# A hybrid encoder layer on one core: first modulation on TensorE, normalisation on three engines, K and Q sums on VectorE, the residual gate 16 chunks later

## The chip, the core and the metric

The kernel runs on one core of a Trainium2 chip. The metric is the device time of one execution in microseconds (us). Five engines work in parallel, each through its own stream of instructions in a fixed order: TensorE (PE in the profile: matrix products; PEld: its weight loads), VectorE (DVE), ScalarE (ACT), GpSimd (POOL), and SyncE (SP), which here only issues DMA transfers. An instruction that waits holds up everything behind it on its engine. Products land in PSUM, 8 banks of 128x512 floats, and a bank must be emptied by VectorE or ScalarE before it is used again.

## The reference

```python
mod = jax.nn.silu(c) @ w_ada[l] + b_ada[l]
shift, scale, gate = jnp.split(mod[:, None, :], 3, axis=-1)
h = _layernorm(x) * (1.0 + scale) + shift
proj = h @ w_in[l]
u, v, z_a, q, k, v_b, z_b = jnp.split(proj, IN_SPLITS, axis=-1)
y_a = _spatial_gating(gelu(u), gelu(v), z_a, ...)   # u * (W_s LN(v) + b) * silu(z_a), 8 groups of 128
y_b = _neighbourhood_attention(q, k, v_b, rpb) * silu(z_b)   # 16 heads of 64
y = jnp.concatenate([y_a, y_b], axis=-1) @ w_out[l]
x = _layernorm(DEEPNORM_ALPHA * x + (1.0 + gate) * y, ln_g[l], ln_b[l])
```

There are 512 tokens, a model width of 2048, and one layer. `w_ada` is 2048x6144, `w_in` 2048x7168, `w_out` 2048x2048, all float32, so that some 126 MB of weights are read once.

## The kernel before, in words

Every float32 weight tile and every activation is split into a rounded part and a rest (`hi` and `lo`), and one product becomes three: hi·hi, hi·lo and lo·hi (`mm3`, line 206). A weight *chunk* is 128x1024 floats (two k tiles of 128 rows by 512 columns): its DMA fills `raw`, ScalarE casts `whi` (line 192), and VectorE or GpSimd subtracts to get `wlo` (line 194). One chunk feeds 24 matmuls of 512 columns, or, for the values and their gate (`VZ`), 24 of 256 columns (line 235) and 12 of 512.

All chunks stand in one list, `plan`, in the order of their use. `pump()` issues their DMAs on SP's queue ahead of use, as long as there is room among 4 `raw` buffers; `split_w()` takes the next one and issues cast and subtraction. The same list holds 32 integers, the *gate steps*: a 128x1024 block of the third part of `w_ada` is loaded into one of two `rawg` buffers, and VectorE adds c times it to `gate1` (line 178). `gate1` is summed over partitions much later (`gate_sum`) and is needed first by the output projection.

The program is staged as follows.

- **Start.** Four token tiles of x are normalised (`first_norm`): VectorE takes statistics, GpSimd computes the factors and scales four quarters (line 412), TensorE transposes them, ScalarE copies them back.
- **Preparation beside the first segments.** For each k tile, `ada_dve` multiplies blocks of `w_ada` (`wada`, six buffers) with c on VectorE (lines 351 and 353), sums the two halves (ScalarE line 357, VectorE line 358), lets TensorE sum over partitions with a column of ones (line 364), and `make_h` forms `h_hi` and `h_lo` (lines 374 to 379). The first two k tiles are done singly, the others in pairs. `advance` deals out these steps among the products by a fixed pace.
- **Segments.** `SEGMENTS` lists k pairs 0, 1, 2, 3, {4,5} and {6,7}. In each, five column groups are worked on: V, U, ZA, VZ0 and KQ0. VZ0 stays in four PSUM banks (`res`); the other groups' partial sums go from two PSUM banks (ring "x") into SBUF with `sum_evac`: for V and U by VectorE (line 440), for ZA and KQ0 by a ScalarE copy (line 437) into a quarter of `gate1` that serves as scratch, and a GpSimd addition (line 438).
- **Last segment**, k pairs {6,7}, in the order KQ0, V, U, VZ0, ZA, with four new banks of ring "x". Beside it runs `sgu`, the spatial gating of the first half: VectorE statistics of V, GpSimd's `rss` (line 119), a scaling (line 524), two GpSimd operations (526, 527), products (533) and VectorE's two operations on their result (534, 537).
- **Three head quarters** q = 1, 2, 3: 16 chunks each, beside the attention of the quarter before. Then V, U and ZA of the second half (24 chunks), the second spatial gating and `gate_sum`, and 32 chunks of the output projection with the final layer norm.

`run(main, side, pace, start)` sets how the side work is dealt out among the products. Below that a scheduler may move an instruction ahead of others on its engine, unless it is wrapped in `pin`, which keeps it in program order. The gate steps begin at plan index 40, the first head quarter, and are spread as 2 per 3 chunks; their VectorE operation is not pinned.

Of the kernel before, what the change touches and what calls it, by code (L numbers as in the profile page):

```python
# [8 lines left out]
F32 = mybir.dt.float32  # L9
F32R = mybir.dt.float32r  # L10
AF = mybir.ActivationFunctionType
# [28 lines left out]

AHEAD, PER_PAIR = 16, 16

LASTS = [0, 0, 1, 1, 1, 1, 1, 0, 1, 0]

PACE_FIRST = (1.5, 18)
# [23 lines left out]
def hybrid_kernel(ctx: ExitStack, tc: tile.TileContext, x, c, w_ada, b_ada_cols, b_gate, w_in,  # L69
# [99 lines left out]
    def split_w():  # L169
# [137 lines left out]
    with tc.tile_pool(name="ph1", bufs=1) as ph1:  # L307
# [32 lines left out]
        def ada_dve(k0, nk):  # L340

            w = nk * P
            step = 4 // nk
            part = [t[:, :2 * w].rearrange("p (s w) -> p s w", s=2) for t in acc_ps]
            for j0 in range(0, NK, step):
                wt = ada_next()
                for j in range(j0, j0 + step):
                    cj = c_sb[:, j:j + 1]
                    acc = part[j % 2]
                    if j < 2:  # L350
                        nc.vector.tensor_scalar(out=acc, in0=wt[:, j - j0], scalar1=cj, scalar2=None, op0=ALU.mult)
                    else:
                        nc.vector.scalar_tensor_tensor(out=acc, in0=wt[:, j - j0], scalar=cj, in1=acc, op0=ALU.mult, op1=ALU.add)  # L353
                pump()
                yield
            even, both = [scratch[i][:, :2 * w].rearrange("p (s w) -> p s w", s=2) for i in range(2)]
            nc.scalar.copy(out=even, in_=part[0])
            nc.vector.tensor_tensor(out=both, in0=part[1], in1=even, op=ALU.add)

            pc = acc_ps[0][:, T - 2:] if nk == 1 else bank()[:, :2 * nk]  # L360
            pc = pc.rearrange("p (s k) -> p s k", s=2)
            for s in range(2):
                for i in range(nk):
                    nc.tensor.matmul(pc[:, s, i:i + 1], lhsT=both[:, s, i * P:(i + 1) * P], rhs=one, start=True, stop=True)
            nc.vector.tensor_tensor(out=modc[:, :, k0:k0 + nk], in0=pc, in1=bada[:, :, k0:k0 + nk], op=ALU.add)
            yield

# [13 lines left out]
        def prepare():  # L381
            for k0, nk in ada_groups:
                yield from ada_dve(k0, nk)
                for kk in range(k0, k0 + nk):
                    make_h(kk, k0 < 2)
                    yield
# [8 lines left out]
        rstd = ph1.tile([P, NT], F32, name="rstd")  # L395
        for n in range(NT):
# [3 lines left out]
        def first_norm(n):  # L400
# [8 lines left out]
            nc.gpsimd.tensor_tensor(out=rstd[:, n:n + 1], in0=rstd[:, n:n + 1], in1=mhalf[:, 0:1], op=ALU.pow)  # L409
            for q in range(4):  # L410
# [19 lines left out]
        def sum_evac(q, i, ps, first):  # L430

            acc = accs[q][0][i]
            if first:
                nc.scalar.copy(out=acc, in_=ps)
            elif q in (ZA, KQ0):
# [6 lines left out]
        def sums(q, wls, i, first):  # L442
# [7 lines left out]
            sum_evac(q, i, ps, first)  # L450
            yield

        def first_segment():
# [11 lines left out]
            for i in range(2):  # L465
                mm3(two[i], wv, i, 1, False, False, True)
                sum_evac(V, i, two[i], True)
                yield
            for i in range(2, 4):
                yield from sums(V, [wv], i, True)  # L470
# [486 lines left out]
```

## Time and profile before

| | |
|---|---|
| median of 3 runs | 963.13 us (961.21 to 964.08) |
| the profiled execution | 963.75 us, its span 962.0 us |
| mean granted TensorE clock | 0.974 of 2.4 GHz |
| busy: PE, DVE, ACT, POOL | 881.7, 592.9, 337.3, 363.5 us |
| read from HBM | 140.6 MB |

Times in the rows below are microseconds from the start of the span. "Idle before" names what ended an engine's wait. A matmul's recorded duration overlaps the next one's, so the distance of starts is the cost of one in a row of many. PEclk is the granted TensorE clock; it has two levels, 1.2 and 2.4 GHz, and a value between is the mean over a stretch.

### The profile page before, as it was taken

How to read it: one execution, taken by the hardware profiler on the slowest of the kernel's cores; microseconds unless marked ns; L12 is line 12 of the kernel's file. 1: busy time of each engine (PE TensorE's matmuls, PEld its weight loads, DVE VectorE, ACT ScalarE, POOL GpSimd, SP SyncE). 2: the span in 40 equal slices, each digit the busy share in tenths (PEclk: the TensorE clock that was granted, in tenths of full speed). 3: DMA queues.
4: the chain of work that ended last, by engine and by line, in shares of the span. 5: the costliest groups of instructions: out<-in, count | busy, mean ns of one | idle time of the engine just before them, and what ended most of it. 6: DMA issues, size and time to landing. Idle time of an engine off the chain costs nothing.

```text
span 962.0 us, 11759 instructions
## 1 busy us (share of the span) xinstructions
PE 881.7 (92%) x4408; PEld 760.7 (79%) x4408; DVE 592.9 (62%) x834; ACT 337.3 (35%) x426; POOL 363.5 (38%) x271
## 2 busy tenths in 40 slices
PE   3699998997985997899999999999999999999994
PEld 3588787886874986689988998899888888888883
DVE  7748768621987875757455745574847843342657
ACT  3364343333531214172516251624245432122300
POOL 5435786367472143434424342434235000000035
PEclk9799999999997998999999999999999999999998
DMA  9969789734626665323233223333232374223313
GB/s 308 311 219 355 243 259 301 239 88 131 197 75 217 205 214 176 99 88 99 89 97 97 91 88 99 88 88 88 75 101 88 115 274 180 89 86 110 110 44 131
DMA packets 107787, 145.59 MB, mean 151 GB/s; under 512 B 6993, under 2 KB 78801, under 8 KB 106961
## 3 DMA queue, kind: packets, MB, share of 16 engines
q1 hardware_dynamic: 103120, 134.25, 43.8%
q10 hardware_dynamic: 4610, 10.59, 3.2%
q8 instruction: 34, 0.56, 0.2%
q14 instruction: 23, 0.19, 0.1%
HBM read 140.62 MB, written 4.19 MB: 151 GB/s over the span
## 4 chain that ended last, share of the span: by engine, by line
PE 57%; DVE 7%; DMA 4%; POOL 3%; issue 2%; ACT 1%; POOLq 0%; DVEq 0%; ACTq 0%
PE psm L222 47%; PE psm L235 5%; DMA rawg<-in_w_ada_dram 4%; DVE gate L178 3%; PE psx L222 1%; DVE s L524 1%; POOL xr L836 1%; POOL xr L837 1%; PE psx L654 1%; PE psx L605 1%; PE psx L606 1%; PE psx L652 1%; DVE wlo L194 1%; PE psx L653 1%; PE psx L533 1%
## 5 line engine op out<-in xcount | busy, mean ns | idle before, releaser
L192 ACT CAST whi<-raw 128x1024 fp32r<-128x1024 f32 x133 | 139.5, 1049 | 328.6 <-PE psm L222 239.6
L194 DVE TENSOR_TENSOR wlo<-raw,whi 128x1024 fp32r<-128x1024 f32 x94 | 126.8, 1349 | 175.4 <-ACT whi L192 172.3
L222 PE MATMUL psm<-h_hi,whi 128*128 128x512 f32 x444 | 175.6, 396 | 0.0
L222 PE MATMUL psm<-h_lo,whi 128*128 128x512 f32 x444 | 174.9, 394 | 0.0
L222 PE MATMUL psm<-h_hi,wlo 128*128 128x512 f32 x444 | 174.5, 393 | 0.0
L194 POOL TENSOR_TENSOR wlo<-raw,whi 128x1024 fp32r<-128x1024 f32 x39 | 94.8, 2437 | 96.6 <-ACT whi L192 80.6
L222 PE MATMUL psm<-whi,h_hi 128*128 128x512 f32 (+1 forms) x296 | 114.7, 388 | 0.0
L222 PE MATMUL psm<-wlo,h_hi 128*128 128x512 f32 (+1 forms) x296 | 114.0, 385 | 0.0
L222 PE MATMUL psm<-whi,h_lo 128*128 128x512 f32 (+1 forms) x296 | 114.0, 385 | 0.0
L222 PEld LDWEIGHTS psm<-h_hi,wlo 128*128 128x128 f32 x444 | 84.5, 190 | 18.2
L222 PEld LDWEIGHTS psm<-h_lo,whi 128*128 128x128 f32 x444 | 84.7, 191 | 15.1
L222 PEld LDWEIGHTS psm<-h_hi,whi 128*128 128x128 f32 x444 | 84.3, 190 | 15.4 <-ACT s L775 0.2
L353 DVE SCALAR_TENSOR_TENSOR ada<-wada,c_sb,ada 128x512 f32<-128x512 f32 (+1 forms) x126 | 79.8, 688 | 19.8 <-DMA wada<-in_w_ada_dram 16.5
L222 PE MATMUL psx<-h_hi,whi 128*128 128x512 f32 x160 | 65.5, 411 | 11.3 <-ACT gate L437 7.8
L119 POOL TENSOR_TENSOR rs<-vareps,mhalf 128x1 f32<-128x1 f32 x4 | 4.4, 1099 | 184.5 <-DVE vareps L118 184.5
L235 PE MATMUL psm<-whi,h_lo 128*128 128x256 f32 x248 | 71.2, 289 | 2.8 <-DVE h_lo L379 2.8
L235 PE MATMUL psm<-wlo,h_hi 128*128 128x256 f32 x248 | 71.1, 287 | 2.7 <-POOL wlo L194 1.9
L235 PE MATMUL psm<-whi,h_hi 128*128 128x256 f32 x248 | 71.4, 288 | 2.4 <-ACT h_hi L374 2.3
L222 PEld LDWEIGHTS psm<-wlo,h_hi 128*128 128x128 f32 x296 | 63.6, 215 | 8.4
L222 PEld LDWEIGHTS psm<-whi,h_lo 128*128 128x128 f32 x296 | 63.4, 214 | 8.5
L222 PEld LDWEIGHTS psm<-whi,h_hi 128*128 128x128 f32 x296 | 63.4, 214 | 8.5
L222 PE MATMUL psx<-h_hi,wlo 128*128 128x512 f32 x160 | 63.5, 397 | 2.3 <-POOL wlo L194 2.3
(196 smaller groups left out, 1668.7 us busy)
## 6 DMA issues: line engine op xcount, KB each, us to landing
wada<-in_w_ada_dram SPq DMA_DIRECT2D x128, 256.0 KB, 5.7
raw<-in_w_in_dram SPq DMA_DIRECT2D x128, 256.0 KB, 3.2
raw<-in_w_in_dram SPq DMA_DIRECT2D x48, 512.0 KB, 3.8
rawg<-in_w_ada_dram SPq DMA_DIRECT2D x32, 512.0 KB, 4.4
raw<-in_w_out_dram SPq DMA_DIRECT2D x32, 512.0 KB, 3.7
xt<-in_x_dram SPq DMA_DIRECT2D x8, 512.0 KB, 8.6
xr<-in_x_dram ACTq DMA_DIRECT2D x4, 1024.0 KB, 9.0
tt<-in_rpb_dram ACTq DMA_DIRECT2D x16, 128.0 KB, 2.5
```

What stands on the lines that cost most here:

```text
L178: nc.vector.scalar_tensor_tensor(out=gate1[:, cs], in0=raw, scalar=c_sb[:, j:j + 1], in1=gate1[:, cs], op0=ALU.mult, op1=ALU.add)
L192: nc.scalar.copy(out=hi, in_=raw)
L194: eng.tensor_tensor(out=low, in0=raw, in1=hi.bitcast(F32), op=ALU.subtract)
L222: nc.tensor.matmul(ps, lhsT=a, rhs=b, start=first and j == 0, stop=last and j == 2)
L235: nc.tensor.matmul(ps[:, t * w:(t + 1) * w], lhsT=a, rhs=b[:, cs], start=first and t == 0 and j == 0, stop=last and t == 1 and j == 2)
L353: nc.vector.scalar_tensor_tensor(out=acc, in0=wt[:, j - j0], scalar=cj, in1=acc, op0=ALU.mult, op1=ALU.add)
L524: nc.vector.tensor_scalar(out=v[n][:, tok(g)], in0=v[n][:, tok(g)], scalar1=mvs[:, g, 0:1], scalar2=rs[:, g:g + 1], op0=ALU.subtract, op1= ...
L533: nc.tensor.matmul(ps[:, tok(n)], lhsT=v[n][:, tok(g)], rhs=wsT[:, g, :], start=True, stop=True)
L605: nc.tensor.matmul(po, lhsT=k2[:, h, keys], rhs=q2[:, h, q], start=True, stop=False)
L606: nc.tensor.matmul(po, lhsT=klo[:, h, keys], rhs=q2[:, h, q], start=False, stop=True)
L652: nc.tensor.matmul(ps[:, q], lhsT=v_hi[:, t, h, :], rhs=hi[:, sl], start=t == 0, stop=False, skip_group_check=True)
L653: nc.tensor.matmul(ps[0:64, q], lhsT=v_lo[:, t, h, :], rhs=hi[:, sl], start=False, stop=False, skip_group_check=True)
```

## The change

1. The first two k tiles' modulation goes to TensorE: `ada_tensor` multiplies each 128x128 block of `w_ada`, as stationary operand, with one column of c, 32 matmuls for each k tile, and VectorE adds the bias straight from PSUM. For the other pairs, `ada_vector` lets the last multiply-add of the even half write SBUF (no ScalarE copy), and the end of one pair (`ada_end`: sum over partitions, `make_h`) comes after the first or second block of the next.
2. `first_norm`'s four quarters go to GpSimd, ScalarE, VectorE and GpSimd (for the last tile VectorE takes the fourth too); GpSimd computes one more factor, `nb`.
3. `sum_evac`: KQ0 is added by VectorE, ZA too in segment 4.
4. The gate steps begin at plan index 56, in place of 40, and are inserted after the second half's chunks are in the plan, so that 48 chunks carry them: those of head quarters 2 and 3, and of V and U. Their VectorE operation is pinned.
5. `pump()` keeps 3 `raw` tiles loaded and not yet split, in place of 4; there are still 4 buffers.
6. `sgu` in the last segment takes PSUM banks of ring "m" in place of "x"; paces and the interleaving at the start (`LASTS`) are set anew.

```diff
+FIRST_GATE = 56
-LASTS = [0, 0, 1, 1, 1, 1, 1, 0, 1, 0]
-PACE_FIRST = (1.5, 18)
+LASTS = [1, 1, 0, 0, 0, 0, 1, 1, 1, 1]
+PACE_FIRST = (1.5, 19)
...
-            room = (RAWG if gate else RAW) - sum(g == gate for g, _ in loaded)
+            room = (RAWG if gate else RAW - 1) - sum(g == gate for g, _ in loaded)
...
-            nc.vector.scalar_tensor_tensor(out=gate1[:, cs], in0=raw, scalar=c_sb[:, j:j + 1], in1=gate1[:, cs],
-                                           op0=ALU.mult, op1=ALU.add)
+            pin(nc.vector.scalar_tensor_tensor(out=gate1[:, cs], in0=raw, scalar=c_sb[:, j:j + 1], in1=gate1[:, cs],
+                                               op0=ALU.mult, op1=ALU.add))
...
-    first_gate = len(plan) - 48
-    for step in range(32):
-        plan.insert(first_gate + (step // 2) * 5 + 3 * (step % 2), step)
     for col in (COL_V, COL_U, COL_ZA):
         plan_group(w_in_v, [(col + 512, 512)], EVEN, "dve")
+    for step in range(32):
+        plan.insert(FIRST_GATE + (step // 2) * 5 + 3 * (step % 2), step)
...
+        def ada_tensor(kk):
+            pc = [t[:, T - 2 + kk:T - 1 + kk] for t in acc_ps]
+            for j0 in range(0, NK, 4):
+                wt = ada_next()
+                for j in range(j0, j0 + 4):
+                    for s in range(2):
+                        nc.tensor.matmul(pc[s], lhsT=wt[:, j - j0, s, :], rhs=c_sb[:, j:j + 1], start=j == 0, stop=j == NK - 1)
+                pump()
+                yield
+            for s in range(2):
+                nc.vector.tensor_tensor(out=modc[:, s, kk:kk + 1], in0=pc[s], in1=bada[:, s, kk:kk + 1], op=ALU.add)
+            yield
...
+                        nc.vector.scalar_tensor_tensor(out=even if j == NK - 2 else acc, in0=wt[:, j - j0], scalar=cj, in1=acc,
+                                                       op0=ALU.mult, op1=ALU.add)
+                if j0 == 2 * (k0 > 4):
+                    yield from before
+            nc.vector.tensor_tensor(out=both, in0=acc_ps[1], in1=even, op=ALU.add)
...
-                nc.gpsimd.tensor_scalar(out=xn[:, cs], in0=xn[:, cs], scalar1=mv[:, n, 0:1], scalar2=rstd[:, n:n + 1],
-                                        op0=ALU.add, op1=ALU.mult)
+                if q == 1:
+                    nc.scalar.activation(out=xn[:, cs], in_=xn[:, cs], func=AF.Identity, scale=rstd[:, n:n + 1], bias=nb[:, n:n + 1])
+                else:
+                    eng = nc.vector if q == 2 or q == 3 == n else nc.gpsimd
+                    eng.tensor_scalar(out=xn[:, cs], in0=xn[:, cs], scalar1=mv[:, n, 0:1], scalar2=rstd[:, n:n + 1],
+                                      op0=ALU.add, op1=ALU.mult)
...
-            elif q in (ZA, KQ0):
+            elif q == ZA and seg < 4:
                 part = scratch[2 + i % 2]
                 nc.scalar.copy(out=part, in_=ps)
                 nc.gpsimd.tensor_tensor(out=acc, in0=part, in1=acc, op=ALU.add)
...
-        steps, taken, total = 0, 0, 11 * (len(EVEN) - 1)
+        steps, taken, total = 0, 0, 12 * (len(EVEN) - 1)
...
-            ps = bank()
+            ps = bank(ring)
...
-    run(last_segment(), sgu(0, acc_v, y_a0, *y_b[1], y_b[0][3]), *PACE_FIRST)
+    run(last_segment(), sgu(0, acc_v, y_a0, *y_b[1], y_b[0][3], "m"), *PACE_FIRST)
```

How the instructions stand on their engines is shown at two places. The first is TensorE's stream from the transposes (before: line 416, after: 444) to the first product of chunks. `ada_111` and `ada_112` are the two PSUM banks of the modulation; line 348 is `ada_tensor`'s matmul. Before:

```order
L416 MATMUL psm<-ident,xt 128x128 x64
L364 MATMUL ada_111<-one,gate_89 128x1 x2
L235 MATMUL psm<-whi,h_hi 128x256
L235 MATMUL psm<-wlo,h_hi 128x256
L235 MATMUL psm<-whi,h_hi 128x256
```

And after:

```order
L444 MATMUL psm<-ident,xt 128x128 x9
L348 MATMUL ada_111<-c_sb,wada 128x1 x4
L348 MATMUL ada_112<-c_sb,wada 128x1 x4
L348 MATMUL ada_111<-c_sb,wada 128x1 x4
L348 MATMUL ada_112<-c_sb,wada 128x1 x4
L237 MATMUL psm<-whi,h_hi 128x256 x2
L224 MATMUL psm<-h_hi,whi 128x512
```

Half of the first k tile's 32 single-column matmuls now stand behind the last transposes. The second k tile's 32 stand behind all the first k tile's products.

The second place is VectorE's stream near the end of the last segment, where `sgu` empties its PSUM banks into `y_b_104` (line 534 before, 562 after) and where ZA's sums are added (727 before, 755 after). Before:

```order
L524 TENSOR_SCALAR s<-s,mvs,rss 128x128 x4
L178 SCALAR_TENSOR_TENSOR gate_89<-rawg,c_sb,gate_89 128x1024 x4
L660 TENSOR_TENSOR v_lo<-vb,v_hi 128x1024
L178 SCALAR_TENSOR_TENSOR gate_89<-rawg,c_sb,gate_89 128x1024
L194 TENSOR_TENSOR wlo<-raw,whi 128x1024
L534 TENSOR_TENSOR y_b_104<-psx,y_b_105 128x512
L178 SCALAR_TENSOR_TENSOR gate_89<-rawg,c_sb,gate_89 128x1024
L537 TENSOR_TENSOR y_a_93<-y_b_104,y_a_93 128x4x128
```

And after:

```order
L688 TENSOR_TENSOR v_lo<-vb,v_hi 128x1024
L196 TENSOR_TENSOR wlo<-raw,whi 128x1024
L562 TENSOR_TENSOR y_b_104<-psm,y_b_105 128x512
L565 TENSOR_TENSOR y_a_93<-y_b_104,y_a_93 128x4x128
L196 TENSOR_TENSOR wlo<-raw,whi 128x1024
```

No gate step is left in this place; in the stream of before, all 32 stand between the end of segment 4 and the second half of head quarter 1, up to four in a row. Now the first stands in the last chunks of quarter 1 and the others singly between the splits and the attention's operations of quarters 2 and 3, and of V and U.

## Rows read from the trace of the kernel before

**Rows 1.** The page's busy tenths of 40 equal slices of the span (24 us each), and the granted clock.

```profile
PE   3699998997985997899999999999999999999994
...
PEclk9799999999997998999999999999999999999998
```

**Rows 2.** Busy time by stage. Columns: stretch, its length, busy us (x instructions) of PE, PEld, DVE, ACT, POOL, then PEclk, DMA share, GB/s. The stretches: start; first products until TensorE runs through; segments 0 to 4; the gap ahead of the last segment; last segment; head quarters 1, 2 and 3; the rest.

```profile
0.00:31.22 31.22, 12.39 (x68) 9.47 (x68) 18.60 (x42) 13.75 (x22) 18.88 (x36) 0.99 1.01 305
31.22:45.27 14.05, 8.99 (x35) 7.28 (x36) 13.04 (x24) 3.17 (x4) 6.97 (x3) 0.74 1.04 338
45.27:227.46 182.19, 173.91 (x817) 148.74 (x817) 112.75 (x171) 75.87 (x109) 105.66 (x62) 0.98 0.75 238
227.46:232.72 5.26, 0.00 (x1) 0.00 (x1) 0.00 (x0) 2.58 (x3) 5.26 (x7) 0.96 0.18 56
232.72:314.93 82.21, 65.23 (x297) 55.77 (x298) 64.95 (x98) 27.81 (x38) 39.72 (x23) 0.90 0.51 162
314.93:429.43 114.50, 102.81 (x563) 89.07 (x562) 77.76 (x86) 39.62 (x48) 42.09 (x31) 0.96 0.51 160
429.43:527.16 97.73, 97.73 (x562) 86.09 (x562) 56.16 (x70) 40.01 (x48) 36.92 (x32) 1.00 0.29 92
527.16:624.89 97.73, 97.73 (x561) 86.11 (x561) 55.55 (x70) 39.76 (x48) 36.94 (x32) 1.00 0.30 92
```

**Rows 3.** Waits of PE between 227 and 430 us: who waited for whom, us in total, times, longest.

```profile
PE psx L533 <- DVE y_b L534: 8.3, 1, 8.3
PE psx L605 <- DVE w L699: 5.6, 1, 5.6
PE psx L222 <- ACT gate L437: 5.3, 1, 5.3
```

**Rows 4.** Waits of DVE in the same stretch.

```profile
DVE gate L178 <- DMA rawg<-in_w_ada_dram: 18.6, 11, 4.3
```

**Rows 5.** Pieces of the chain of waits that ended last: start, us, what. First the gate steps around 290 us, then runs of products at full rate (120 of 512 columns, 24 of 256 columns, 8 passes of one `sgu` group).

```profile
288.54 3.90 DMA rawg<-in_w_ada_dram
...
292.52 2.75 DVE gate L178
295.29 4.91 DMA rawg<-in_w_ada_dram
...
429.43 2.90 PE psm L235 x24
...
497.25 27.28 PE psm L222 x120
...
748.00 0.89 PE psx L533 x8
```

**Rows 6.** The gate step's VectorE operation: all of them, with min/median/max duration in ns, first and last start.

```profile
L178 DVE SCALAR_TENSOR_TENSOR gate<-rawg,c_sb,gate x32: 1236/1286/3330, 242.0 to 383.8; 128x1024 f32<-128x1024 f32 x32
```

**Rows 7.** Instructions of POOL and ACT in order of time ahead of the last segment: start, us, engine, line, out<-in, and in brackets the idle time before it.

```profile
229.61 1.11 POOL L596 TENSOR_TENSOR bm<-tt,mask 128x256 f32<-128x256 f32 x2
230.69 4.67 POOL L194 TENSOR_TENSOR wlo<-raw,whi 128x1024 fp32r<-128x1024 f32 x2
231.14 1.04 ACT L192 CAST whi<-raw 128x1024 fp32r<-128x1024 f32 x1 [1.68 <-POOL bm L596]
232.09 0.58 ACT L437 COPY gate<-psx 128x512 f32<-128x512 f32 x1
```

**Rows 8.** Instructions of POOL in order of time in the last segment, around `sgu`'s chain.

```profile
265.24 1.03 POOL L119 TENSOR_TENSOR rss<-vareps,mhalf 128x4 f32<-128x4 f32 x1
...
274.35 1.28 POOL L527 TENSOR_TENSOR s<-s,y_b 128x512 f32<-128x512 f32 x1
275.59 2.35 POOL L194 TENSOR_TENSOR wlo<-raw,whi 128x1024 fp32r<-128x1024 f32 x1
```

**Rows 9.** Instructions in order of time at the start: scaling of the last token tile, last transposes, first cast, the modulation's sum, `h_hi` of the first k tile, VectorE's scaling of the transposed x, and a later sum over partitions of four matmuls.

```profile
23.32 3.02 POOL L412 TENSOR_SCALAR xt<-xt,mv,rstd 128x512 f32<-128x512 f32 x4
24.14 2.91 PE L416 MATMUL psm<-ident,xt 128*128 128x128 f32 x16 [1.27 <-POOL xt L412]
28.75 4.68 POOL L194 TENSOR_TENSOR wlo<-raw,whi 128x1024 fp32r<-128x1024 f32 x2 [2.42 <-ACT whi L192]
28.83 1.06 ACT L192 CAST whi<-raw 128x1024 fp32r<-128x1024 f32 x1
30.36 0.81 ACT L374 ACTIVATE h_hi<-xt,modc 128x512 fp32r<-128x512 f32 x1 [0.47 <-DVE modc L365]
31.28 2.44 DVE L375 TENSOR_SCALAR xt<-xt,modc 128x512 f32<-128x512 f32 x1 [0.49 <-ACT h_hi L374]
66.49 1.05 PE L364 MATMUL psx<-one,gate 128*128 128x1 f32 x8
```

**Rows 10.** Groups of DVE's instructions between 45.27 and 227.46 us: busy us, mean ns of one, then idle time just before them and what ended it.

```profile
L440 DVE TENSOR_TENSOR s<-psx,s 128x512 f32<-128x512 f32 x16 | 11.0, 686 | 5.2 <-PE psx L222 5.1
L365 DVE TENSOR_TENSOR modc<-psx,bada 128x4 f32<-128x4 f32 x7 | 1.1, 161 | 21.1 <-PE psx L364 21.0
```

**Rows 11.** Waits of PE between 45.3 and 227 us.

```profile
PE psx L222 <- ACT gate L437: 4.1, 3, 1.6
PE psx L222 <- DVE s L440: 3.3, 3, 1.4
```

**Rows 12.** Waits of SP's DMA queue between 0 and 100 us.

```profile
SPq L165 <- POOL wlo L194: 20.0, 5, 10.7
```

More of the change, by code (lines that the diff above doesn't have):

```diff
@@ L338, in hybrid_kernel, with ada_vector @@
         acc_ps = [ps_a.tile([P, T], F32, name=f"ada{i}") for i in range(2)]
[L340 to L345, printed above, removed]
-                wt = ada_next()
-                for j in range(j0, j0 + step):
-                    cj = c_sb[:, j:j + 1]
-                    acc = part[j % 2]
+        def ada_tensor(kk):
+            pc = [t[:, T - 2 + kk:T - 1 + kk] for t in acc_ps]
+            for j0 in range(0, NK, 4):
+                wt = ada_next()
+                for j in range(j0, j0 + 4):
[6 more added lines that the diff above has]
+            yield
+        def ada_vector(k0, before):
+            even, both = scratch[:2]
+            for j0 in range(0, NK, 2):
+                wt = ada_next()
+                for j in range(j0, j0 + 2):
+                    cj, acc = c_sb[:, j:j + 1], acc_ps[j % 2]
                     if j < 2:
@@ L381, in prepare @@
         def prepare():
[L382 to L386, printed above, removed]
+            for kk in range(2):
+                yield from ada_tensor(kk)
+                make_h(kk, True)
+                yield
+            before = iter(())
+            for k0 in EVEN[1:]:
+                yield from ada_vector(k0, before)
+                before = ada_end(k0)
+            yield from before
         prep = prepare()
@@ L395, in hybrid_kernel @@
         rstd = ph1.tile([P, NT], F32, name="rstd")
+        nb = ph1.tile([P, NT], F32, name="nb")
         for n in range(NT):
@@ L428, in hybrid_kernel, with sum_evac @@
         turn[0] = 4
-        def sum_evac(q, i, ps, first):
+        def sum_evac(q, i, ps, seg):
             acc = accs[q][0][i]
-            if first:
+            if seg == 0:
                 nc.scalar.copy(out=acc, in_=ps)
-            elif q in (ZA, KQ0):
+            elif q == ZA and seg < 4:
                 part = scratch[2 + i % 2]
@@ L440, in sum_evac, with sums @@
                 nc.vector.tensor_tensor(out=acc, in0=ps, in1=acc, op=ALU.add)
-        def sums(q, wls, i, first):
+        def sums(q, wls, i, seg):
             ps = bank()
@@ L449, in sums @@
                     yield
-            sum_evac(q, i, ps, first)
+            sum_evac(q, i, ps, seg)
             yield
@@ L466, in first_segment @@
                 mm3(two[i], wv, i, 1, False, False, True)
-                sum_evac(V, i, two[i], True)
+                sum_evac(V, i, two[i], 0)
                 yield
             for i in range(2, 4):
-                yield from sums(V, [wv], i, True)
+                yield from sums(V, [wv], i, 0)
             for q in SEGMENTS[0][1][2:]:
@@ L473, in first_segment @@
                 for i in range(4):
-                    yield from sums(q, wls, i, True)
+                    yield from sums(q, wls, i, 0)
         def segment(s):
@@ L484, in segment @@
                     for i in range(4):
-                        yield from sums(q, wls, i, False)
-        steps, taken, total = 0, 0, 11 * (len(EVEN) - 1)
+                        yield from sums(q, wls, i, s)
+        steps, taken, total = 0, 0, 12 * (len(EVEN) - 1)
         for s in range(len(SEGMENTS) - 1):
@@ L503, in hybrid_kernel, with sgu @@
     nc.scalar.dma_start(out=gate1[0:1, :], in_=b_gate)
-    def sgu(half, v, y, gB, bB, wsT, bs, sv):
+    def sgu(half, v, y, gB, bB, wsT, bs, sv, ring="x"):
         hs = slice(half * 512, (half + 1) * 512)
```

21 lines of the change are left out of this document (11 added, 10 removed).

## The prediction

> **What bounds the kernel now.** I read the slices first, then the stages, then the waits of TensorE inside the stages that fall short. The slices [rows 1] show TensorE full from the eighteenth slice (408 us) to the last but one. The gaps stand at the start and between 216 and 408 us, and there the granted clock falls too. The stages [rows 2] give the measure. Head quarters 2 and 3 do the same work (16 chunks and one quarter's attention) and take 97.73 us each, with TensorE busy throughout at full clock. That is TensorE's own price. Head quarter 1, with the same products, takes 114.50 us: 16.8 too many.
>
> The last segment can be priced likewise. 120 passes of 512 columns take 27.28 us, 24 of 256 columns 2.90 us, one `sgu` group of products 0.89 us [rows 5]; a pass is 0.227 and 0.121 us. The segment has 8 chunks of 24 long passes (43.6), two VZ0 chunks of 24 short and 12 long (11.3) and four `sgu` groups (3.6): 58.5 us. It takes 82.21 [rows 2], so 23.7 too many. Ahead of it stand 5.26 us in which TensorE does nothing. Together these three places hold 45.8 us over TensorE's own time, lost clock included.
>
> What ends the waits there? In 227 to 430 us the longest [rows 3] are for the emptying of `sgu`'s banks (8.3), an attention result (5.6) and the copy of a K/Q sum (5.3). The first two are VectorE's. VectorE itself waited 18.6 us, 11 times, for gate blocks still on their way [rows 4], and the chain shows it around 290 us: a 3.90 us transfer, two gate steps, a 4.91 us transfer [rows 5]. The gate step has no hurry, but in VectorE's fixed order everything behind it waits: the splits, the emptying of banks, the attention's steps. The 5.3 us are another case. The last K/Q copy runs at 232.09 us, behind a cast that waited for GpSimd, which was at the attention's tables and splits [rows 7]; TensorE starts as it ends.
>
> **The change part by part.** The sum goes against the profiled execution, 963.75 us; the median is 963.13, so a difference carries over.
>
> *Gap ahead of the last segment.* VectorE now adds the K/Q sums from PSUM itself, one operation of 0.69 us [rows 10] in place of a ScalarE copy and a GpSimd addition, and VectorE was idle there (0.00 busy) [rows 2]. One operation and the signals about it remain, some 1.0 us: −4.3, between −5.3 and 0, should the copy's place be taken by a late modulation step.
>
> *Last segment.* No gate step is left on VectorE, so its DMA waits and the 13 of the 32 steps that stand here, of 1.29 us each [rows 6], go. What is late next is GpSimd: in `sgu` four `rss` of 1.03 us, eight operations of 1.28 and the splits of 2.35 between them [rows 8] make 4 × 1.03 + 8 × 1.28 + 2 × 2.35 = 19.1 us from the first `rss`, and V's chain has the 22 us of U and VZ0 for it, with one more split ahead. That just fits, and the two splits of ZA stand behind it. I leave 3 us of waits (0 to 13): the segment becomes 61.5 us, −20.7 (−23.7 to −10). The other ring costs nothing: the four banks of `res` are free once VZ0 is emptied, and `sgu`'s first product stands behind 12 of ZA's passes; if that cover failed, TensorE would wait for ScalarE's few operations, inside the 3 us. The new start of the side work, 19 for 18, is one step of 1.4 us and is not priced.
>
> *Head quarter 1.* Without gate steps but for the first at its end it is quarters 2 and 3 of before: from 114.50 to 98.7, one us left for the turn into it: −15.8 (−16.8 to −8).
>
> *Quarters 2 and 3, V and U.* Here 32 gate steps are added where TensorE is full. VectorE has room: 56.16 of 97.73 us busy [rows 2]; a quarter gets 10.7 steps, at the median 13.8 us, at most 35 at the longest seen [rows 6]: 70 to 91 of 97.7. What is queued behind one are the splits, of which two chunks (11 us) are always ahead, and attention steps, whose slack I cannot read. The blocks are two ahead, some 2.5 chunks or 14 us, against transfers of 3.9 to 4.9 us [rows 5], at 92 GB/s now and 160 with them, where the start ran at 305 [rows 2]. So the DMA wait, the dear part, should not recur. Pinning keeps the steps from bunching. SP issues 32 more transfers in this stretch and none in the old one; each waits for the step two before it, done by then. I take +2 (0 to +10; a gain is excluded, since TensorE has no gap there).
>
> On the length of a step the trace and a page can be weighed. The steps range from 1.24 to 3.33 us [rows 6]. The Trainium skill, SBUF — State Buffer, section Who interferes with whom, says that a VectorE instruction with two SBUF inputs contends with a GpSimd instruction that reads SBUF, one blocking the other. The gate step has two such inputs; by that rule it would be longer beside GpSimd's work, and the range of the row fits it. By the rule the term would lie above the median's; by the row alone it lies between 13.8 and 35 us a quarter, as taken.
>
> *Start.* Four token tiles lose half of GpSimd's scaling; it was 3.02 us for the last one [rows 9], after the factors. With two quarters on VectorE and one each on ScalarE and GpSimd the last transposes come perhaps 2 us sooner than 27.05, at 25. VectorE's price for a quarter is not shown; the nearest row is 2.44 us for 512 elements beside a GpSimd split [rows 9], and at that price for two the transposes would end at 28. Behind them stand 16 of the single-column matmuls. The nearest row has 8 passes for 4 matmuls in 1.05 us [rows 9], 0.114 from start to start taking a last pass of 0.25; 32 passes are 3.7 us. Bias, `h_hi` (0.81) and the first cast, now behind `h_hi` on ScalarE (1.05), bring the first product to about 31, as now. The second cast and two splits of 2.35 bring `wlo` of the second chunk to 36, the first tile's products end at 37.5, the second tile's 64 passes take 7.3, and with `h_hi`, `h_lo` TensorE runs through from about 47.5, where it was 45.27. So +2 (−4 to +7): single-column passes take the place of waiting, and what VectorE is spared was hidden behind ScalarE's order. GpSimd's extra factor, four of 0.2 us, lies within this.
>
> *Segments 0 to 4.* Waits of TensorE for banks are 4.1 and 3.3 us [rows 11], the first of them the copy that is removed. VectorE gains 20 additions of 0.69 us [rows 10], 13.8 us on 112.75 of 182.19 [rows 2], 69%. It loses 21.0 us of waiting for the sum over partitions [rows 10], since that end now stands behind the next pair's first blocks. On SP the loads of `raw` waited 20.0 us for GpSimd's splits [rows 12], with the `wada` loads behind them; with one load less ahead the buffer is free at issue. Clock: the stretch ran at 0.98. I take −5 (−10 to +4, where more additions stand behind multiply-adds that wait for `wada`).
>
> Sum: −4.3 − 20.7 − 15.8 + 2 + 2 − 5 = −41.8. 963.75 becomes 921.9; against the median 921.3. I say 922.
>
> **The rivals.** *The second k tile is late and the DMA held back.* The six `wada` buffers are freed only as TensorE gets to them, at 37 to 45 us, so the transfers stand still after 30 us. For it: the first 190 us move most of the bytes, at 238 GB/s over segments 0 to 4 beside 338 just before [rows 2]. Against: there is room up to that rate. Start +7 and segments +4: 14 us more, 936.
>
> *GpSimd bounds the last segment.* The 19.1 us chain slips behind splits, as `rss` did. Then only 10 of 23.7 come back: 10.7 more, 932.6.
>
> *The start gains as well.* Transposes spread over three engines, TensorE kept at work so that the clock (0.74 in 31 to 45 us) [rows 2] stays up, fewer SP waits: −4 and −10 in place of +2 and −5: 911.
>
> *The other side: each pinned gate step lands on TensorE's path.* If every step delays a split or an attention result that TensorE waits for, 32 × 1.29 = 41.2 us come back, and with the old DMA wait spread over them, 18.6 [rows 4], 59.8 in place of 2: 980. It decides against the change from 43.8/32 = 1.37 us of TensorE per step. For it: quarter 1 lost 16.8 us with 19 of the steps. Against: those came in bunches, with DMA waits. That the gate steps don't move is no rival: the order shows them moved.
>
> **How the numbers follow.** Forecast 0.40, second k tile late 0.20, GpSimd 0.17, start gains 0.17, other side 0.06. The forecast's own range is 913 to 931. For 8 in 10 I reach up to 945, over the two slower cases at once, and down to 906. Within 0.3% (2.9 us) is what can't be told from no change; the forecast, the three nearer rivals and their sums are all faster by more. Faster 0.94; of the other side 0.01 falls within 0.3%, since its price passes through it, and 0.05 above.
>
> **What would show it.** Right: the gap ahead of the last segment near 1 us, that segment 60 to 65, head quarter 1 near 98, no wait of VectorE for `rawg`, quarters 2 and 3 at 98 to 99 with a full clock. Wrong: quarters 2 and 3 above 103, with TensorE waiting for VectorE; or TensorE running through only after 50 us; or segments 0 to 4 longer than 182 us with TensorE waiting for VectorE's additions; or a last segment above 68 with the waits on GpSimd.

## The result and the profile after

The changed kernel takes 937.91 us (median of 4 runs, 936.25 to 940.47) against 963.38 before on the same chip: a ratio of 0.974, 95% interval 0.971 to 0.977. That is 25.5 us less, where 41.8 were forecast. The profiled execution has a span of 934.7 us, 27.3 less than the 962.0 before. Where these lie, the stages show (columns as in [rows 2]; the stretches are the same eight, and the rest):

```profile
0.00:38.06 38.06, 21.21 (x128) 20.57 (x129) 14.74 (x32) 15.03 (x25) 12.05 (x29) 0.83 0.94 286
38.06:55.22 17.16, 15.88 (x89) 14.79 (x89) 0.73 (x4) 1.76 (x3) 4.93 (x2) 0.70 0.55 169
55.22:234.30 179.08, 174.25 (x824) 149.59 (x824) 129.50 (x194) 63.14 (x85) 90.77 (x49) 0.99 0.76 245
234.30:235.18 0.88, 0.01 (x1) 0.03 (x1) 0.69 (x1) 0.00 (x0) 0.88 (x2) 1.00 0.29 93
235.18:302.79 67.61, 62.43 (x297) 54.17 (x297) 42.24 (x86) 30.36 (x41) 36.74 (x22) 0.95 0.35 104
302.79:401.62 98.83, 98.01 (x561) 85.98 (x560) 53.65 (x66) 39.62 (x47) 36.27 (x31) 1.00 0.32 97
401.62:499.35 97.73, 97.73 (x562) 86.10 (x561) 72.11 (x80) 38.66 (x45) 38.62 (x32) 1.00 0.48 151
499.35:597.08 97.73, 97.73 (x562) 86.09 (x561) 74.09 (x81) 39.67 (x48) 41.77 (x32) 1.00 0.49 151
597.08:934.70 337.62, 323.12 (x1514) 278.38 (x1512) 209.16 (x289) 95.78 (x113) 76.92 (x49) 0.98 0.36 123
```

Against [rows 2], stage by stage, beside the terms of the prediction:

| stage | before | after | measured | predicted |
|---|---|---|---|---|
| start, until TensorE runs through | 45.27 | 55.22 | +9.95 | +2 (−4 to +7) |
| segments 0 to 4 | 182.19 | 179.08 | −3.1 | −5 (−10 to +4) |
| gap | 5.26 | 0.88 | −4.4 | −4.3 (−5.3 to 0) |
| last segment | 82.21 | 67.61 | −14.6 | −20.7 (−23.7 to −10) |
| head quarter 1 | 114.50 | 98.83 | −15.7 | −15.8 (−16.8 to −8) |
| quarters 2, 3 and the rest | 532.57 | 533.08 | +0.5 | +2 (0 to +10) |

The mark "TensorE runs through" is the end of its last wait in the start, as in the prediction. Before, that wait stands behind the first seven passes of the second k tile, and after, ahead of all of them (817 and 824 passes in segments 0 to 4), so that for equal work the start lost more than 9.95 us and segments 0 to 4 gained more than 3.1. The second k tile's first product came at 42.50 us before and at 55.22 after.

The gate steps now lie where TensorE is full, and quarters 2 and 3 are still 97.73 us at full clock: VectorE's busy time there rose from 56 to 72 and 74 us, and TensorE lost nothing. The trace's view of the gate step's line (count, min/median/max duration in ns, first and last start) has no wait of VectorE for a `rawg` block, where there were 18.6 us [rows 4]:

```profile
L180 DVE SCALAR_TENSOR_TENSOR gate<-rawg,c_sb,gate x32: 1239/1276/3158, 389.0 to 679.2; 128x1024 f32<-128x1024 f32 x32
```

**The start** went wrong. TensorE in order of time (start, us, line; in the rows of line 348, x counts passes, two for each of its float32 matmuls; dots stand for rows left out):

```profile
24.82 1.01 PE L444 MATMUL psm<-ident,xt 128*128 128x128 f32 x6
25.62 1.71 PE L348 MATMUL ada<-c_sb,wada 128*128 128x1 f32 x8
27.19 2.16 PE L444 MATMUL psm<-ident,xt 128*128 128x128 f32 x9
29.14 6.83 PE L348 MATMUL ada<-c_sb,wada 128*128 128x1 f32 x32
38.06 0.80 PE L237 MATMUL psm<-whi,h_hi 128*128 128x256 f32 x2 [2.09 <-ACT whi L194]
...
44.67 9.45 PE L348 MATMUL ada<-c_sb,wada 128*128 128x1 f32 x64
55.22 0.58 PE L237 MATMUL psm<-whi,h_hi 128*128 128x256 f32 x1 [1.10 <-ACT h_hi L392]
```

And four stretches of it, and the one behind it (stretch, its length, TensorE's busy time and passes, granted clock, DMA share, GB/s):

```profile
25.62:29.14 3.52, 3.52 (x18) 0.50 1.18 293
29.14:35.97 6.83, 6.83 (x33) 0.50 0.88 257
44.67:49.50 4.83, 4.83 (x44) 0.98 0.33 109
49.50:54.12 4.62, 4.62 (x22) 0.50 0.76 217
55.22:59.90 4.68, 4.68 (x18) 0.54 0.52 160
```

32 passes of the first k tile take 6.83 us, 0.213 each; the second tile's take 0.115 each up to 49.5 us (42 in 4.83; the row's 44 counts its neighbours at the edges) and 0.21 behind it (22 in 4.62). So a pass costs 0.115 us at 2.4 GHz and 0.21 at 1.2. The clock fell to 1.2 GHz twice: by 25.62 us, where such passes alternate with transposes, and at 49.5 us, where TensorE, recorded as busy throughout, did nothing else. Weight loads fill these stretches: in order of time, PEld has

```profile
44.44 9.59 PEld L348 LDWEIGHTS ada<-c_sb,wada 128*128 128x128 f32 x64
```

so that each pass costs the load of its 128x128 block and not its single column. The Trainium skill, TensorE: Matmul & The Clock Gate, section LDWEIGHTS (loading the stationary operand), gives the number of columns over 1.2 in ns, which for 128 columns makes an estimate of 107 ns; the 0.115 us at full clock agree with it to 8%, and the 0.21 us at half clock are twice that.

Others wait meanwhile. VectorE waits for the sums, and SP's DMA queue for the `wada` buffers (total, times and longest, in the first 60 and 70 us):

```profile
DVE modc L352 <- PE ada L348: 28.2, 4, 14.0
```

```profile
SPq L320 <- PE ada L348: 13.2, 6, 4.9
```

The second is what holds the `wada` buffers: the DMA share is 0.55 between 38 and 55 us, where it was 1.04 in the same stage before [rows 2].

**The last segment** keeps 9.1 us over the 58.5 of its bare products. TensorE's waits in it, both between 279 and 286 us:

```profile
PE psx L224 <- POOL wlo L196: 2.9, 1, 2.9
PE psx L224 <- ACT whi L194: 2.2, 1, 2.2
```

What stands ahead of them on ScalarE, and then on GpSimd and VectorE (start, us, in brackets the idle time before):

```profile
275.40 0.63 ACT L762 ACTIVATE y_a<-y_a 128x512 f32<-128x512 f32 x1 [11.45 <-DVE y_a L755]
...
280.60 0.63 ACT L762 ACTIVATE y_a<-y_a 128x512 f32<-128x512 f32 x1 [2.32 <-DVE y_a L755]
281.13 1.03 ACT L194 CAST whi<-raw 128x1024 fp32r<-128x1024 f32 x1
```

```profile
280.89 1.27 POOL L554 TENSOR_TENSOR s<-s,y_b 128x512 f32<-128x512 f32 x1 [1.53 <-DVE s L552]
282.24 1.28 POOL L555 TENSOR_TENSOR s<-s,y_b 128x512 f32<-128x512 f32 x1
283.48 5.70 POOL L196 TENSOR_TENSOR wlo<-raw,whi 128x1024 fp32r<-128x1024 f32 x2
```

```profile
271.83 2.92 DVE L552 TENSOR_SCALAR s<-s,mvs,rss 128x128 f32<-128x128 f32 x3 [1.83 <-POOL rss L121]
274.68 0.68 DVE L755 TENSOR_TENSOR y_a<-psx,y_a 128x512 f32<-128x512 f32 x1
```

VectorE adds U's banks only between `sgu`'s scalings, ScalarE's Gelus of U wait for that, a cast stands behind the Gelus, and a split behind `sgu`'s last operation on GpSimd. Of the 9.1 us, 5.1 are these two waits; behind them the clock falls, and the mean granted clock is 0.69 in 281 to 292 us (columns as in the five stretches above):

```profile
281.00:292.00 11.00, 6.86 (x21) 0.69 0.29 90
```

### The profile page after: what moved, and what is told of

Its sections match the earlier page's. It is cut to its first block, busy times and chain, and to the rows that moved or that the text cites. A ratio compares the mean times of both kernels' runs of the same rounds, so it can differ in the third digit from the quotient of the medians.

```text
span 934.7 us, 11916 instructions
## 1 busy us (share of the span) xinstructions
PE 890.4 (95%) x4528; PEld 775.7 (83%) x4528; DVE 596.9 (64%) x827; ACT 324.0 (35%) x401; POOL 339.0 (36%) x246
## 4 chain that ended last, share of the span: by engine, by line
PE 82%; POOL 4%; DVE 4%; issue 4%; DMA 3%; SPq 1%; ACT 1%; POOLq 0%; DVEq 0%; ACTq 0%
PE psm L224 52%; PE psx L224 15%; PE psm L237 8%; DMA wada<-in_w_ada_dram 2%; SPq L320 1%; POOL wlo L196 1%; PE ada L348 1%; POOL xr L864 1%; DVE s L552 1%; PE psx L682 1%; PE psx L634 1%; PE psx L633 1%; PE psx L680 1%; DMA xt<-in_x_dram 1%; POOL xr L865 1%
## 5 line engine op out<-in xcount | busy, mean ns | idle before, releaser
L196 DVE TENSOR_TENSOR wlo<-raw,whi 128x1024 fp32r<-128x1024 f32 x94 | 131.4, 1399 | 160.8 <-ACT whi L194 155.2
L365 DVE SCALAR_TENSOR_TENSOR ada<-wada,c_sb,ada 128x512 f32<-128x512 f32 x91 | 64.0, 749 | 7.4 <-DMA wada<-in_w_ada_dram 3.9
```

Of the source, the lines that this page charges most:

```text
L196: eng.tensor_tensor(out=low, in0=raw, in1=hi.bitcast(F32), op=ALU.subtract)
L365: nc.vector.scalar_tensor_tensor(out=even if j == NK - 2 else acc, in0=wt[:, j - j0], scalar=cj, in1=acc, op0=ALU.mult, op1=ALU.add)
```

## The experiments

Ratios are to the kernel before, run on the same chip, with 95% intervals.

**The start: four kernels.** In all of them the rest of the change stays, except that the two kernels with VectorE's modulation of both tiles (e2, e8) also have before's interleaving at the start, `LASTS`. For the modulation `ada_single` is before's `ada_dve` for one k tile; in the mixed kernel (e3) it has no ScalarE copy.

```diff
-LASTS = [1, 1, 0, 0, 0, 0, 1, 1, 1, 1]
+LASTS = [0, 0, 1, 1, 1, 1, 1, 0, 1, 0]                                                  # e2, e8
...
-                yield from ada_tensor(kk)
+                yield from ada_single(kk, True)                                         # e2, e8
+                yield from (ada_single(kk, False) if kk else ada_tensor(kk))            # e3
...
-                if q == 1: (ScalarE) else: (VectorE or GpSimd)
+                nc.gpsimd.tensor_scalar(out=xn[:, cs], in0=xn[:, cs], ...)              # e7, e8
```

> The changed kernel with the modulation of the first two k tiles on VectorE again (16 scaled adds per tile into two banks, ScalarE's copy of one bank, one add, one pass per half), as before the change; the normalisation stays on three engines. Theory (the lost time of the start is TensorE's own: 32 and 64 single-column passes and the transposes that stand between them): TensorE runs through at 43 to 47 us instead of 55.2, and the time is 925 to 931 us (937.9 less 8 to 12). Rival 1 (the spread normalisation makes the start late, because VectorE and ScalarE now do it beside their other work): the start stays at 53 to 56 and the time at 936 to 940. Rival 2 (VectorE, with the modulation and a part of the scaling, is now the late one): a start of 47 to 53, 931 to 937 us.

> The changed kernel with the whole scaling of the normalisation on GpSimd again; TensorE keeps the modulation of the first two k tiles. Theory (TensorE's passes are late by themselves and the normalisation is not to blame): the scalings of GpSimd take about 3.0 us per quarter beside transfers as they did before (ends about 24 us, and the transposes about 25 to 29), so the start ends at 55 to 59 us and the time is 937 to 942, not better than the changed kernel. Rival 1 (the spread normalisation makes the start late): a start of 45 to 50, 928 to 934 us.

> The changed kernel with both parts of the start undone: scaling on GpSimd, first two k tiles on VectorE with ScalarE's copy; all else (sums of K and Q, gate steps, rings, pace of preparation) as in the changed kernel. Theory (the start costs the change 10 us, all of it from the two edits of the start): the start is as before, 44 to 47 us, and the time 926 to 931. Rival (the start's 10 us come from elsewhere in the change, from the transfers that now come in another order or the one raw buffer fewer): a start over 50 and a time of 934 to 940. Beside the kernel with only the modulation undone, it tells what the three engines' normalisation is worth: 0 to 3 us by the theory.

> The changed kernel with the first k tile's modulation on TensorE and the second's on VectorE (without ScalarE's copy). Theory (TensorE's single-column passes are the late work, and the second tile's 64 cost most, 9.45 us and the wait for them): the second product is fed about when VectorE's 16 adds are done, the start ends at 46 to 50 us, and the time is 928 to 934. If only the first tile's 32 passes were the cost, which the trace does not say, the start would stay above 52 and the time at 936 or more.

| scaling on | modulation of tiles 1, 2 on | TensorE runs through | median us | ratio |
|---|---|---|---|---|
| three engines (the change) | TensorE, TensorE | 55.22 | 937.9 | 0.974 (0.971 to 0.977) |
| GpSimd (e7) | TensorE, TensorE | 59.34 | 936.8 | 0.973 (0.971 to 0.974) |
| three engines (e2) | VectorE, VectorE | 47.22 | 926.3 | 0.962 (0.960 to 0.964) |
| GpSimd (e8) | VectorE, VectorE | 46.97 | 924.5 | 0.960 (0.958 to 0.962) |
| three engines (e3) | TensorE, VectorE | 51.41 | 925.1 | 0.961 (0.959 to 0.962) |

Taking the modulation off TensorE gives 12 us with either normalisation; the normalisation makes no difference that can be measured with either modulation. The theory holds in direction, and the rivals that blame the normalisation or other parts of the change fall. The ranges were less good: e8 (924.5) and e3 (925.1) came out below 926 and 928, and e3's start, 51.41 us, was over the 46 to 50 expected. The 3.0 us "per quarter" in e7's expectation are those of all four quarters of a token tile [rows 9]. With GpSimd scaling all and TensorE modulating, TensorE runs through 4 us later and still the time is the same; 2.5 us of it are left where the last segment begins (237.69 us for 235.18), and I cannot lay the rest to one row. Where e8's gain sits, its first stages show (start to the first product, to running through, to 60 us, to the end of segment 4; then the last segment):

```profile
0.00:32.16 32.16, 14.11 (x68) 11.04 (x68) 18.75 (x42) 13.86 (x22) 19.29 (x36) 0.84 1.01 301
32.16:46.97 14.81, 9.94 (x38) 8.11 (x38) 14.59 (x26) 3.17 (x4) 6.55 (x3) 0.78 1.07 349
46.97:60.00 13.03, 12.07 (x55) 10.46 (x56) 11.17 (x17) 6.45 (x11) 2.86 (x2) 1.00 1.04 350
60.00:223.10 163.10, 157.52 (x761) 136.14 (x759) 113.22 (x171) 54.67 (x73) 83.28 (x46) 1.00 0.74 235
...
223.98:290.35 66.37, 61.70 (x297) 53.32 (x298) 42.22 (x86) 30.37 (x41) 36.66 (x22) 0.95 0.35 106
```

TensorE runs through 8.3 us sooner than in the changed kernel, and at full clock from there, where the changed kernel has 0.54 for another 4.7 us; the DMA share stays above 1.0 in place of 0.55. Of the 12.8 us between the two spans 8.3 lie in the start, 3.0 in segments 0 to 4 (176.13 us against 179.08) and 1.2 in the last segment.

The mixed kernel gains nearly all though TensorE runs through only 3.8 us sooner. In its stages the other part is in segments 0 to 4, and with it goes the stall of transfers (SP's wait for TensorE falls from 13.2 to 5.2 us); its second tile's first product came at 47.49 us, 7.7 sooner, ahead of a last wait for `h_lo`:

```profile
38.41:51.41 13.00, 9.48 (x36) 7.79 (x36) 12.06 (x25) 3.60 (x4) 9.63 (x4) 0.76 0.90 283
51.41:60.00 8.59, 8.33 (x31) 7.50 (x32) 8.56 (x14) 3.06 (x5) 2.38 (x1) 0.80 0.86 267
```

```profile
SPq L320 <- PE ada L348: 5.2, 2, 2.7
```

So it is the second tile's 64 passes, with the buffers they hold, that cost; the first tile's cost nothing that these times show. How much is TensorE's own time in the passes and how much the transfers held back, these kernels don't separate, since each takes away both.

**The gate steps alone**: the kernel before, with only part 4 of the change.

```diff
-    first_gate = len(plan) - 48
-    for step in range(32): ...
     for col in (COL_V, COL_U, COL_ZA): ...
+    for step in range(32):
+        plan.insert(56 + (step // 2) * 5 + 3 * (step % 2), step)
...
+            pin(nc.vector.scalar_tensor_tensor(out=gate1[:, cs], ...))
```

> The kernel before with one part of the change only: the 32 residual gate steps from place 56 of the plan on, in program order on VectorE. Theory (the gate steps in the last segment and quarter 1 held VectorE up behind their transfers; in quarters 2 and 3 they hide): quarter 1 falls from 114.5 us to 98 to 100 and the last segment from 82.2 to 67 to 73, start and gap stay (45.3 and 5.3), so 963 less 25 to 31 = 932 to 938 us; the change would then owe this part nearly all of its gain. Rival (the steps only shift their waits): quarters 2 and 3 rise above 97.7 by as much as quarter 1 falls, 950 to 965 us.

933.3 us, ratio 0.968 (0.965 to 0.971). Its start, segments 0 to 4, gap, last segment and quarter 1:

```profile
0.00:46.19 46.19, 22.77 (x104) 18.10 (x104) 31.64 (x66) 17.03 (x26) 25.91 (x38) 0.85 1.01 309
46.19:227.07 180.88, 172.88 (x817) 148.13 (x817) 112.59 (x171) 75.61 (x109) 105.64 (x61) 0.99 0.75 240
227.07:232.39 5.32, 0.00 (x1) 0.01 (x1) 0.00 (x0) 2.57 (x3) 5.32 (x7) 0.78 0.16 55
232.39:301.08 68.69, 63.51 (x297) 54.57 (x297) 42.69 (x86) 28.32 (x38) 37.52 (x23) 0.94 0.33 100
301.08:399.60 98.52, 98.36 (x564) 86.35 (x563) 53.67 (x67) 40.15 (x47) 36.56 (x31) 1.00 0.32 97
```

The last segment and quarter 1 fall as in the full change, the gap stays. The rest of the span, from quarter 2 on, takes 532.5 us, as before, so the rival falls. This part alone is worth 30 us, more than the whole change.

**The gate steps not pinned.**

```diff
-            pin(nc.vector.scalar_tensor_tensor(out=gate1[:, cs], ..., op1=ALU.add))
+            nc.vector.scalar_tensor_tensor(out=gate1[:, cs], ..., op1=ALU.add)
```

> The changed kernel with the gate steps left free for the scheduler's order (place 56 kept). On VectorE some of them then stand in the last segment again, ahead of K and Q's last group sums and of the sgu's scalings. Theory (what cost in the kernel before was VectorE's wait for each step's transfer in front of work that TensorE waits for): waits of VectorE for rawg appear and the last segment grows by 5 to 20 us, 943 to 958 us. Rival (place 56 alone is the gain, order is idle): 936 to 940 us.

963.7 us, ratio 1.000 (0.998 to 1.003): worse than the theory said, and the rival falls. The same view of the step's line, with its waits:

```profile
L180 DVE SCALAR_TENSOR_TENSOR gate<-rawg,c_sb,gate x32: 1241/1284/3521, 231.8 to 377.6; 128x1024 f32<-128x1024 f32 x32
...
  DMA rawg<-in_w_ada_dram: 27.6, 10
```

The scheduler took the steps from place 56 back to 231.8 us, ahead of the work that TensorE waits for, and VectorE waited 27.6 us for their transfers. So the place in the plan brings little without the pin, and 26 of the gate steps' 30 us hang on the pin. A pin at the old place, 40, was not tried, so what the pin is worth without the later place stays open.

**K and Q's sums on ScalarE and GpSimd again**, and with them ZA's of segment 4.

```diff
-            elif q == ZA and seg < 4:
+            elif q in (ZA, KQ0):
```

> The changed kernel with the group sums of K and Q on ScalarE and GpSimd again (and ZA's in every segment), as before the change. Theory (the 5.3 us ahead of the last segment stood behind ScalarE's copies): the gap goes from 0.9 back to 4 to 6 us, segments 0 to 4 stay within 2 us, and the time is 940 to 944 us. Rival 1 (VectorE's sums are no better for the rest, and the gap closes by the gate's move): 936 to 939. Rival 2 (with no sums on VectorE, its modulation of the later k tiles runs ahead and segments 0 to 4 gain 2 to 4): 935 to 938.

944.8 us, ratio 0.980 (0.976 to 0.983), 6.9 us above the changed kernel, though the intervals of the two ratios just overlap. TensorE's waits for ScalarE's copies are back, though not in one place as the theory had it: only 1.6 us stand just ahead of the last segment and 1.9 some 5 us before, the other two at 146 and 176 us:

```profile
PE psx L224 <- ACT gate L465: 6.3, 4, 1.9
```

Both rivals fell: segments 0 to 4 with the gap take 185.6 us against 180.0 in the changed kernel. The start, which this edit does not reach, was 2.0 us later in that execution, so the sums are worth some 5 to 7 us. Of the gap's 5.3 us only 1.6 came back in its old place, and 1.9 ahead of it: what else closes it is not shown.

**The last segment: low parts on VectorE.**

```diff
-            plan_group(w_in_v, firsts[q], [2 * pair for pair in pairs], "pool")
+            plan_group(w_in_v, firsts[q], [2 * pair for pair in pairs], "dve" if pairs[-1] == 7 and q in (VZ0, ZA) else "pool")
```

> The changed kernel with the low parts of four chunks of the last segment (VZ0's and ZA's) made by VectorE instead of GpSimd. On VectorE, U's bank sums then also come ahead of half of the sgu's scalings. Theory (the 9.1 us that the last segment takes over its bare products are two waits, 2.2 us for ScalarE's cast behind U's Gelus and 2.9 for GpSimd's low part behind the sgu's products, and the half clock after them): both waits go and the last segment falls from 67.6 us to 59 to 62, 930 to 934 us. Rival (VectorE now serves the sgu late, and TensorE waits for y_b and s at the sgu's products, as before the change): the last segment stays at 66 or more, 937 to 943 us.

930.9 us, ratio 0.966 (0.963 to 0.969). The last segment:

```profile
232.60:295.69 63.09, 60.68 (x296) 53.44 (x297) 40.38 (x90) 30.48 (x41) 31.23 (x18) 0.97 0.36 111
```

Both waits went, and 4.5 us of that segment's time, which stays above the 59 to 62 expected: a new wait of 2.4 us came, of `sgu`'s first product for GpSimd's `s`, which is the rival's kind in small. Another 2.6 us of the 7.4 between the spans lie ahead of the segment, where this edit does not reach; 1.4 of them are in the start, where the clock fell later in this execution (0.67 in 26 to 28 us, against 0.50 in the changed kernel's). So the edit itself is worth some 4.5 us and not 7.

**Casts ahead of U's Gelus.** U's Gelus are emitted beside VZ0's second chunk, and they and the last segment's casts are pinned.

```diff
+        if BEFORE_LAST < at[1] <= BEFORE_LAST + 10:
+            pin(cast)
...
+                    if last:
+                        for acc in accs[U][0]:
+                            pin(nc.scalar.activation(out=acc, in_=acc, func=AF.Gelu))
...
-                        else:
+                        elif q == V:
```

> The changed kernel with U's four Gelus emitted later and the last segment's casts kept in program order on ScalarE, so that two casts no longer stand behind U's Gelus; GpSimd keeps the low parts, and two of these still stand behind the sgu's last product there. Theory (the waits for ScalarE's cast and for GpSimd's low part are two chains, both from VectorE's late sgu scalings): the 2.2 us wait goes and the 2.9 us wait takes over part or all of it, 935 to 938.5 us. Rival (ScalarE's order is the single cause, GpSimd's low part was late only because its cast was): both waits go, 930 to 933 us.

936.8 us, ratio 0.972 (0.970 to 0.975), no measurable gain. The cast's wait is gone, and the other took it over in full:

```profile
PE psx L226 <- POOL wlo L198: 5.4, 1, 5.4
```

So the rival falls: there are two chains, and GpSimd's, with its splits behind `sgu`'s last operation, ends last.

**`sgu`'s products in ring "x" again.**

```diff
-    run(last_segment(), sgu(0, acc_v, y_a0, *y_b[1], y_b[0][3], "m"), *PACE_FIRST)
+    run(last_segment(), sgu(0, acc_v, y_a0, *y_b[1], y_b[0][3]), *PACE_FIRST)
```

> The changed kernel with the sgu's four product banks taken from the ring of the last segment's own banks again instead of the ring of four m banks. Theory (in the changed kernel VectorE empties a bank soon, and TensorE waits for none): 0 to +2 us, 937 to 940. Rival (the sgu's banks were part of the 8.3 us wait for y_b in the kernel before, and their new ring is part of the gain): the last segment or quarter 1 grows by 4 to 8 us, 942 to 946 us.

936.3 us, ratio 0.972 (0.970 to 0.974): the ring is no part of the gain.

**Both corrections together.** e8's start, and then e3's, with the low parts of VZ0 and ZA on VectorE.

> Both corrections together: normalisation on GpSimd and first two k tiles on VectorE as before the change, and the low parts of VZ0 and ZA in the last segment on VectorE; all else as changed. If the late start and the last segment's two waits are separate losses, the gains add: 937.9 less 13.4 (start) less 7.0 (lows) = 917.5, 914 to 921 us. If the start only moved work that the later stages wait for anyway, or the two share a cause, 922 or more.

> The same with the other start: normalisation on three engines, the first k tile's modulation on TensorE, the second's on VectorE. By the same sum 937.9 less 12.8 less 7.0 = 918.1, 914 to 922 us. Against the run beside it, it tells whether anything of the changed start is worth keeping: by the theory no, a difference under 2 us.

920.8 us with before's start, ratio 0.956 (0.954 to 0.959), and 921.6 with the mixed one, 0.957 (0.955 to 0.959). Both beat the kernel before and the changed one; between them there is no difference that can be measured. The sums were 917.5 and 918.1, 3 us less; they took 7.0 us for the low parts. With the 4.5 us that these gave in the last segment the sums are 920.0 and 920.6, so the gains add. The first one's last segment reads as that of the low parts alone, 63.19 us:

```profile
223.34:286.53 63.19, 60.79 (x296) 53.45 (x297) 40.64 (x90) 30.74 (x41) 31.05 (x17) 0.97 0.37 111
```

## Why the prediction was right and wrong

The direction and the wide range (906 to 945) held, but the time was 15.9 us above the forecast and outside the forecast's own range (913 to 931). Of its signs of being right, the gap, quarter 1, the missing waits for `rawg` and quarters 2 and 3 at full clock came, and the last segment (67.61 us for 60 to 65) did not; of its signs of being wrong one came, TensorE running through only after 50 us. By its own steps:

- *Gap, quarter 1, quarters 2 and 3*: right to 2 us, and quarters 1 to 3 by the mechanism named. The gate steps alone bring quarter 1 down and leave the gap at 5.32; with K and Q's old sums the waits for ScalarE's copies return, 6.3 us of them, but only 3.5 at the gap or just ahead of it, so the gap's mechanism is shown in part. The rival of the other side, each gate step landing on TensorE, showed nothing of its price. On the length of a step: the six longer ones of the changed kernel (2.4 to 3.2 us) all ran beside a GpSimd instruction, and none of the 12 that ran beside none took over 1.29 us; 14 others overlapped one and took no longer than 1.31. What I passed over in half a sentence ("pinning keeps the steps from bunching") carries 26 us: without the pin the place does not keep them out of the last segment.
- *Start*: the step that failed, "32 passes are 3.7 us" and "the second tile's 64 passes take 7.3". The price of 0.114 was read from 8 passes at full clock, and it held at full clock (0.115). But here the clock fell: the 32 all ran at half of it and took 6.83 us, and so did 22 of the 64, which took 9.45. The passes of earlier `wada` blocks also stood between the last transposes, and the clock fell there, so that these ended about 29.3 us, not 25 to 28, though the last scaling did end sooner (at 23.8 us, before the change at 26.3). The first product came at 38.06, not at 31: 4.1 us from that, 3.1 from the clock in the 32 passes. The other 2.2 us come from the second tile's passes, less 1.6 that I had reckoned too much behind them. I had bounded the term at +7; the bound left out the clock. VectorE's price for a scaling, where I feared 2.44 us, was 0.55, and GpSimd's extra factor took 0.52 us, not 0.2.
- *Last segment*: the mechanism was right, and the term was mis-sized: I left 3 us over the bare products and there were 9.1, of which 5.1 were waits and the rest mostly the clock that fell behind them (0.69 in 281 to 292 us). "The two splits of ZA stand behind it" named the queue on GpSimd; that VectorE would add U's banks between `sgu`'s scalings, and so hold ScalarE's casts, I had not read from the order.
- *Segments 0 to 4*: −3.1 for −5, within its bounds. With the start undone they take 176.13 us, −6.1. I take it from this that the term itself was near and that the slow start took half of it back, with its transfers and its clock and with the passes that fall on the other side of the mark; no run separates these.
- *Rivals*: 936 was the time of "second k tile late, DMA held back", and its premise is seen: SP waited 13.2 us for TensorE, and the mixed kernel, which frees the second tile's buffers on VectorE, gets 12.8 us back. That the time matches to 2 us is in part chance, since segments 0 to 4 did not grow by the rival's 4 us but fell by 3.1, while the start cost 8 us more than forecast and the last segment 6. "GpSimd bounds the last segment" came in at 6 of its 10.7 us.

The parts on their own: the gate steps −30.3 us (added to the kernel before), and, each taken out of the changed kernel, K and Q's sums −6.9, the first modulation on TensorE +12 to +13, the other two tested parts nothing: −24 to −25, against −25.5. The agreement is closer than the spread of the runs warrants. The pace of preparation and the `raw` tile fewer were not tried, nor `LASTS` by itself.

## What to carry to other kernels

A side task with no deadline is moved by place and by order together; where a scheduler may bring it forward, the place in a list decides nothing by itself, so read the order and the waits for its transfer. A matrix-vector product on an idle TensorE costs a weight load for each block, it fills TensorE's in-order queue in front of what comes next, and its price must be taken at the clock of that moment. When one of several waits in a row is removed, look on each engine for the next queue that feeds the same instruction.

## What was not expected of the hardware

Single-column passes did not keep TensorE's clock up: between 44.67 and 54.12 us TensorE is recorded as busy throughout, with nothing else, and the granted clock fell to 1.2 GHz at 49.5 us; with it a pass went from 0.115 to 0.21 us, and the clock stayed low through a wait of 1.1 us and another 4.7 us of full-width products (0.54 in 55.2 to 59.9 us). It fell within the second tile's 64 passes in e7 and e9 as well, where they took 9.88 and 9.80 us. No run isolates the cause: the mixed kernel has a clock of 0.80 in 51.4 to 60 us without the second tile's passes, and with before's start it is 1.00 in 47 to 60 us.
